# Four 4 KB-row transfers in place of eight 2 KB-row ones at the opening of a two-layer trunk kernel

## The chip, the cores and the metric

The kernel runs on one core of a Trainium2 chip. A core has a matrix engine (TensorE, PE in the profile, with its weight loads as PEld), a vector engine (VectorE, DVE), a scalar engine (ScalarE, ACT), a general engine (GpSimd, POOL), and a sync engine (SyncE, SP) that here only issues transfers. Sixteen DMA engines move data from the chip's main memory (HBM) into the on-chip memory (SBUF). TensorE writes into banks of an accumulator memory (PSUM). Each engine works through its own instruction list in order and waits on semaphores for the others.

The metric is the device time of one execution in microseconds, the median of a few runs.

## The reference

The reference is a trunk of two layers over 256 latent tokens and 256 context tokens of width 1024. Each layer modulates an RMS-normalised stream, projects it, sends it through a convolution branch, an attention branch and gates, and then through a gated MLP. What the change touches is only the very beginning: the first norm, and the first projection that follows it.

```python
def rmsnorm(x, g):
    xf = x.astype(jnp.float32)
    y = xf * lax.rsqrt(jnp.mean(xf * xf, axis=-1, keepdims=True) + EPS)
    return (y * g.astype(jnp.float32)).astype(x.dtype)
...
    s_lat = jax.nn.silu(c)
    s_ctx = jax.nn.silu(c_ctx)
    for l in range(DEPTH):
        mod = (s_lat @ w_ada[l] + b_ada[l])[:, None, :]
        sh1, sc1, g1, sh2, sc2, g2 = jnp.split(mod, 6, axis=-1)
...
        h = modulate(rmsnorm(x, norm1_g[l]), sh1, sc1)
        p = h @ w_in[l]
```

## The kernel before

The stream is kept transposed: eight tiles `x[0]` to `x[7]`, each of 128 channels (partitions) by 512 tokens in float32, the latent tokens (`LAT`) in the first 256 columns and the context tokens (`CTX`) in the last 256. In HBM each tile is a block of 128 rows of 2 KB.

Weights come as units of 128 partitions by 1024 columns in float32 (512 KB, rows of 4 KB). They land in one of four `raw` buffers, ScalarE makes a rounded copy `whi` (L168, L751, L757 and others), VectorE the remainder `wlo` (L169, L754), and every product runs as three matrix products, high by high, high by low and low by high (`mm3`, L187 to L189; for the value projection `v_tile`, L723). For some units the remainder is made by an accumulating transfer that GpSimd issues (L206 to L208).

The opening runs like this:

- SP issues the eight stream tiles (L595), then two units of modulation weights (`wada`, L155), then the first value unit in two halves of 256 KB (`rv`, L747), then the first GLU unit (`rg`, L155), then modulation weights for the next channels.
- The sum of squares over the channels is built pairwise. Even tiles are squared on ScalarE (L606), odd ones on VectorE (L603), which then adds the pair (L604). In the last pair both engines share the odd tile: ScalarE squares its `LAT` half (L598), VectorE its `CTX` half (L599), and VectorE adds each half to the even tile's square (L601). TensorE sums each pair over the partitions by products with a column of ones (`sum0`, L590, four products a pair, `CTX` columns first). A product with both operands in plain float32 appears in the trace as two PE instructions.
- Then come the modulation products for the first channels (`ada_half`, L220, two units), ScalarE's copy of them (L239), transposes (L246), the root on VectorE and GpSimd (L366, L368), its transposes (L374), the modulation and gain (L251 to L256), the modulated stream `h` (L388 on VectorE, L389 on ScalarE, L390 on VectorE), and the first value products (L723).
- Filler products `busy(n)` (L137) multiply an identity matrix into a bank that is overwritten later. They keep TensorE at work while it has nothing to do. Eleven stand at the start, two after the first pair's sums, one before the last pair's, two and five further on.

TensorE's order in the opening is fixed by the function `queued`, which makes each piece follow the one before it. Elsewhere the order of each engine's list is set by a scheduler that works from the program's order and its own estimates, so an edit at one place can move a neighbour. Each transfer of SP and ScalarE raises one of eight semaphores in turn (DMAHW0 to DMAHW7 in the lists below), and a transfer is issued only when the last one with the same semaphore has landed. SP issues in order, so what stands behind a waiting transfer waits too.

From k = 1 on, a stage of the opening makes one tile of `h`, its value products and its share of the GLU products, and brings two units of modulation weights for the next tile. The place they land in comes free when TensorE has used the units before. After eight stages the first layer goes on with the query and key units (`T_Q`, `T_K`), whose first loads are issued during the last stages.

Of the kernel before, what the change touches and what calls it, by code (L numbers as in the profile page):

```python
# [8 lines left out]
F32 = mybir.dt.float32  # L9
# [6 lines left out]
P = 128  # L16
D = 1024
KD = D // P
DEPTH = 2
S = 256  # L20
# [24 lines left out]
U_GLU0, U_V, U_IN, U_NA, U_CO, U_WO, U_UP, U_DN = 0, 2, 6, 36, 40, 44, 52, 96  # L45
# [8 lines left out]
def trunk(ctx: ExitStack, tc: tile.TileContext, xt, cvec, crow, wall, wada, params, bias_t, rope_t, out):  # L54
    nc = tc.nc
    pe, act, dve, pool, sp = nc.tensor, nc.scalar, nc.vector, nc.gpsimd, nc.sync
# [3 lines left out]
    xp = ctx.enter_context(tc.tile_pool(name="x", bufs=1))  # L60
    wp = ctx.enter_context(tc.tile_pool(name="w", bufs=1))
    hp = ctx.enter_context(tc.tile_pool(name="h", bufs=1))
    tp = ctx.enter_context(tc.tile_pool(name="tmp", bufs=1))
# [4 lines left out]
    def nm(s):  # L68
        uid[0] += 1
        return f"{s}_{uid[0]}"  # L70
# [6 lines left out]
    def tmp(w=512):  # L77
        return tp.tile([P, w], F32, tag="t", bufs=5, name=nm("t"))
# [56 lines left out]
    def busy(n):  # L135
        for _ in range(n):
            mm = pe.matmul(sl(warm, 0), ident, ident, start=True, stop=True)  # L137
        return mm


    queue = [busy(11)]

    def queued(f, *a):
        with tc.issue_after(queue[-1].ins):
            queue.append(f(*a))
# [171 lines left out]
        dve.scalar_tensor_tensor(a, mod2(l, part, k)[:, :ns], 1.0, g, ALU.add, ALU.mult)  # L317


    x = [xp.tile([P, 2 * S], F32, name=f"x{k}") for k in range(KD)]  # L320

    class SumSq:

# [268 lines left out]

    ada0 = psum("po")
    for k in range(KD):
        sp.dma_start(x[k], xt[k])  # L595
        q = tmp()
        if k == KD - 1:
            act.activation(q[:, LAT], x[k][:, LAT], AF.Square)  # L598
            dve.tensor_tensor(q[:, CTX], x[k][:, CTX], x[k][:, CTX], ALU.mult)  # L599
            for c in (CTX, LAT):  # L600
                dve.tensor_tensor(q[:, c], q[:, c], prev[:, c], ALU.add)  # L601
        elif k % 2:
            dve.tensor_tensor(q, x[k], x[k], ALU.mult)  # L603
            dve.tensor_tensor(q, q, prev, ALU.add)  # L604
        else:
            act.activation(q, x[k], AF.Square)  # L606
        if k % 2:
            if k == KD - 1:
                queued(busy, 1)
            queued(sum0, q, k == 1, k == KD - 1)  # L610
            if k == 1:
                queued(busy, 2)
        prev = q
    for u in range(2):
        queued(ada_half, ada0, u, raw_unit(wada[0, u]))
# [2 lines left out]
    for l in range(DEPTH):  # L618
# [5 lines left out]
        with ExitStack() if last else start as e1a:  # L624
# [75 lines left out]
            with ExitStack() as e1b:  # L700
# [27 lines left out]
                if l == 0:  # L728
# [14 lines left out]
                    rv = wp.tile([P, UW], F32, tag="raw", bufs=4, name=nm("raw"))  # L743
                    wv = [wp.tile([P, UW], F32R, tag=t, bufs=4, name=nm(t)) for t in ("whi", "wlo")]
                    cuts = [slice(i * 512, (i + 1) * 512) for i in range(2)]
                    for c in cuts:
                        sp.dma_start(rv[:, c], wall[l, U_V][:, c])  # L747
                    rg = raw_unit(wall[l, U_GLU0])
                    wg = [wp.tile([P, UW], F32R, tag=t, bufs=4, name=nm(t)) for t in ("whi", "wlo")]
                    with tc.issue_after(lastev[0].ins):  # L750
# [575 lines left out]
```

## Time and profile before

| What | Value |
|---|---|
| median of 3 runs | 1106.7 us (1106.16 to 1108.9) |
| the profiled execution's own time | 1108.29 us |
| its span in the profile | 1106.5 us |
| PE busy | 1094.5 us, 99% of the span |
| first value product starts | 15.76 us |
| stream tiles | 8 transfers of 256 KB, median 4.2 us from issue to landing |
| data moved | 209.26 MB, 189 GB/s in the mean |

All times inside the kernel count from the first instruction. The profiled execution took 1.8 us more than its span, and 1.6 us more than the median of the runs. A busy TensorE is not a TensorE at its peak: where it waits shows in the idle time before a group and in the chain of work that ended last, not in the busy share.

### The profile page before, as it was taken

The numbers are of one execution on the slowest core, as the hardware profiler recorded it, in microseconds if no ns is written. First come the engines' busy times: TensorE is split into PE (matmuls) and PEld (weight loads), VectorE is DVE, ScalarE is ACT, GpSimd is POOL, SyncE is SP. The second block draws the span as 40 slices with busy tenths as digits, with TensorE's granted clock in tenths as the row PEclk, the third lists the DMA queues.
The fourth block names the chain that finished last, engine by engine and source line by source line (L and its number), as shares of the span: only waits on it lengthen the run. The fifth ranks groups of instructions, "written<-read, shape, count | busy, mean of one in ns | idle before, by whom it ended". The sixth has DMA issues, their size and how long they took to land.

```text
span 1106.5 us, 18047 instructions
## 1 busy us (share of the span) xinstructions
PE 1094.5 (99%) x6896; PEld 951.2 (86%) x6896; DVE 896.3 (81%) x1630; ACT 567.9 (51%) x943; POOL 42.9 (4%) x59
## 2 busy tenths in 40 slices
PE   9999999999999999999999999999999999999997
PEld 7787777888889888888888888989889999999997
DVE  5568898989998788888898556789799888988773
ACT  4458767445324544343433223544676667666642
POOL 1011110011000000000000000000000000000000
PEclk9999999999999999999999999999999999999998
DMA  9988673988843445544557656557644484655771
GB/s 364 290 212 224 153 163 106 278 246 221 264 134 115 125 140 173 146 159 153 171 185 225 215 176 191 185 185 210 193 127 142 151 275 151 206 189 176 229 261 57
DMA packets 60230, 209.26 MB, mean 189 GB/s; under 512 B 7280, under 2 KB 7536, under 8 KB 60144
## 3 DMA queue, kind: packets, MB, share of 16 engines
q1 hardware_dynamic: 55104, 190.77, 53.4%
q0 software_dynamic: 4752, 17.30, 8.2%
q8 instruction: 54, 0.88, 0.3%
q14 instruction: 32, 0.26, 0.1%
q10 hardware_dynamic: 288, 0.04, 0.0%
HBM read 187.63 MB, written 1.05 MB: 171 GB/s over the span
## 4 chain that ended last, share of the span: by engine, by line
PE 87%; DVE 4%; ACT 3%; DMA 3%; SPq 1%; issue 1%; DVEq 0%; ACTq 0%
PE main L187 25%; PE main L189 25%; PE main L188 25%; PE main L723 4%; DMA raw<-in_wall 2%; SPq L715 1%; PE sc L187 1%; PE sc L188 1%; PE sc L189 1%; DVE wlo L169 1%; PE po L220 1%; PE po L563 1%; ACT whi L168 1%; DVE cb L659 1%; PE sc L480 1%
## 5 line engine op out<-in xcount | busy, mean ns | idle before, releaser
L187 PE MATMUL main<-h,whi 128*128 128x256 f32 (+1 forms) x1328 | 447.3, 337 | 0.0
L189 PE MATMUL main<-h,wlo 128*128 128x256 f32 (+1 forms) x1328 | 443.5, 335 | 1.2 <-DVE wlo L169 1.1
L188 PE MATMUL main<-h,whi 128*128 128x256 f32 (+1 forms) x1328 | 442.5, 334 | 0.1
L168 ACT CAST whi<-raw 128x1024 fp32r<-128x1024 f32 (+1 forms) x211 | 217.7, 1036 | 243.2 <-DMA raw<-in_wall 120.3
L169 DVE TENSOR_TENSOR wlo<-raw,whi 128x1024 fp32r<-128x1024 f32 (+1 forms) x211 | 253.1, 1207 | 90.8 <-ACT whi L168 87.7
L187 PEld LDWEIGHTS main<-h,whi 128*128 128x128 f32 x1328 | 249.5, 188 | 30.4 <-issue 2.2
L189 PEld LDWEIGHTS main<-h,wlo 128*128 128x128 f32 x1328 | 249.4, 188 | 30.2 <-DVE wlo L169 2.0
L188 PEld LDWEIGHTS main<-h,whi 128*128 128x128 f32 x1328 | 249.8, 188 | 28.5 <-DVE h L390 0.5
L659 DVE SCALAR_TENSOR_TENSOR cb<-u,par,cb 128x512 f32<-128x512 f32 (+1 forms) x240 | 144.2, 618 | 2.8
L187 PE MATMUL main<-fh,whi 128*128 128x256 f32 (+1 forms) x386 | 123.0, 319 | 0.0
L188 PE MATMUL main<-fl,whi 128*128 128x256 f32 (+1 forms) x386 | 122.9, 318 | 0.0
L189 PE MATMUL main<-fh,wlo 128*128 128x256 f32 (+1 forms) x386 | 122.9, 318 | 0.0
L293 DVE CUSTOM_DVE_ANT_0 t<-raw,sb,par 128x1024 bf16<-128x1024 f32 x72 | 91.5, 1279 | 0.3 <-ACT sb L273 0.3
L188 PEld LDWEIGHTS main<-fl,whi 128*128 128x128 f32 x386 | 72.7, 188 | 5.6
L189 PEld LDWEIGHTS main<-fh,wlo 128*128 128x128 f32 x386 | 72.7, 188 | 5.6
L187 PEld LDWEIGHTS main<-fh,whi 128*128 128x128 f32 x386 | 72.7, 188 | 5.5
L1053 ACT ACTIVATE t<-main,par 128x512 f32<-128x512 f32 (+1 forms) x82 | 50.8, 669 | 37.6 <-PE main L189 37.6
L293 DVE CUSTOM_DVE_ANT_0 t<-own,sb,par 128x1024 bf16<-128x1024 f32 x48 | 60.4, 1280 | 1.7 <-DMA own<-in_wada 1.7
L206 ACT CAST whi<-raw 128x1024 fp32r<-128x1024 f32 x33 | 34.6, 1050 | 49.8 <-PE main L188 42.3
L1054 DVE SCALAR_TENSOR_TENSOR t<-main,par,t 128x510 f32<-128x510 f32 (+1 forms) x82 | 47.6, 616 | 9.4 <-ACT t L1053 9.1
L1057 DVE SCALAR_TENSOR_TENSOR t<-main,par,t 128x510 f32<-128x510 f32 (+1 forms) x82 | 46.7, 611 | 0.0
L389 ACT ACTIVATE h<-t,mod 128x256 fp32r<-128x256 f32 x56 | 25.1, 501 | 34.8 <-DVE t L388 34.7
(215 smaller groups left out, 1262.9 us busy)
## 6 DMA issues: line engine op xcount, KB each, us to landing
raw<-in_wall SPq DMA_DIRECT2D x239, 512.0 KB, 4.3
raw<-in_wada SPq DMA_DIRECT2D x64, 512.0 KB, 4.5
wlo<-raw POOLq DMA_DIRECT2D x33, 512.0 KB, 5.2
own<-in_wada SPq DMA_DIRECT2D x24, 512.0 KB, 5.6
bias<-in_bias_t SPq DMA_DIRECT2D x8, 520.0 KB, 5.3
row<-in_wada SPq DMA_DIRECT2D x8, 512.0 KB, 4.8
sb<-in_crow SPq DMA_DIRECT2D x5, 512.0 KB, 5.0
x<-in_xt SPq DMA_DIRECT2D x8, 256.0 KB, 4.2
```

What stands on the lines that cost most here:

```text
L168: act.copy(hi[:, c], r[:, c])
L169: dve.tensor_tensor(lo[:, c], r[:, c], hi[:, c].bitcast(F32), ALU.subtract)
L187: pe.matmul(ps, w[0], xh, start=start, stop=False)
L188: pe.matmul(ps, w[0], xl, start=False, stop=False)
L189: pe.matmul(ps, w[1], xh, start=False, stop=stop)
L206: act.copy(hi, r)
L293: dve.tensor_tensor_reduce(tmp().bitcast(BF16), r, v, 1.0, pr(l, BADA + n, 1), ALU.mult, ALU.add, mods[l][:, n, s : s + 1])
L659: dve.scalar_tensor_tensor(cb[j], src, w, cb[j], ALU.mult, ALU.add)
L723: mm = pe.matmul(pv[t], h1[n == 1][k][:, c], w[n == 2][:, b], start=k + n == 0, stop=k == KD - 1 and n == 2)
L1053: act.activation(c, pv_, AF.Identity, bias=pr(l, FDB + t, 1), scale=w[1])
L1054: dve.scalar_tensor_tensor(c[:, :, 1:], pv_[:, :, : S - 1], w[0], c[:, :, 1:], ALU.mult, ALU.add)
L1057: dve.scalar_tensor_tensor(c[:, :, : S - 1], pv_[:, :, 1:], w[2], c[:, :, : S - 1], ALU.mult, ALU.add)
```

## The change

The stream arrives as four tiles of two channel blocks each, with rows of 4 KB; the host lays the input out to match, and `x[k]` becomes a view of half a tile. The first value unit comes in one transfer of 512 KB. The first burst of fillers shrinks from eleven to eight, the one after the first pair's sums from two to one, and the one before the last pair's sums goes. The square of tile 6 goes to a buffer of its own (`ss`) in place of one of the five rotating ones.

```diff
-    queue = [busy(11)]
+    queue = [busy(8)]
...
-    x = [xp.tile([P, 2 * S], F32, name=f"x{k}") for k in range(KD)]
+    x2 = [xp.tile([P, 2, 2 * S], F32, name=f"x{k}") for k in range(KD // 2)]
+    x = [t[:, i] for t in x2 for i in range(2)]
...
     for k in range(KD):
-        sp.dma_start(x[k], xt[k])
-        q = tmp()
+        if k % 2 == 0:
+            sp.dma_start(x2[k // 2].rearrange("p i t -> p (i t)"), xt[k // 2])
+        q = tp.tile([P, 512], F32, tag="ss", name=nm("ss")) if k == KD - 2 else tmp()
...
         if k % 2:
-            if k == KD - 1:
-                queued(busy, 1)
             queued(sum0, q, k == 1, k == KD - 1)
             if k == 1:
-                queued(busy, 2)
+                queued(busy, 1)
...
-                    for c in cuts:
-                        sp.dma_start(rv[:, c], wall[l, U_V][:, c])
+                    sp.dma_start(rv, wall[l, U_V])
...
-        "xt": np.ascontiguousarray(xs.T.reshape(KD, P, 2 * S)),
+        "xt": np.ascontiguousarray(xs.T.reshape(KD // 2, 2, P, 2 * S).transpose(0, 2, 1, 3)).reshape(KD // 2, P, 4 * S),
```

On SP, the list from the last stream tiles to the first GLU unit, with the semaphores waited for. `raw_169` and `raw_175` (now `raw_156` and `raw_162`) are the first modulation units, `raw_234` (now `raw_221`) is the value unit, `raw_239` (now `raw_225`) the GLU unit. Before:

```order
L595 DMA x_115<-in_xt 128x512
L595 DMA x_116<-in_xt 128x512 [waits DMAHW0_49]
L595 DMA x_117<-in_xt 128x512 [waits DMAHW1_49]
L155 DMA raw_169<-in_wada 128x1024 [waits DMAHW2_49]
L155 DMA raw_175<-in_wada 128x1024 [waits DMAHW3_49]
L747 DMA raw_234<-in_wall 128x512 [waits DMAHW4_49]
L747 DMA raw_234<-in_wall 128x512 [waits DMAHW5_49]
L155 DMA raw_239<-in_wall 128x1024 [waits DMAHW6_49]
```

And now:

```order
L597 DMA x_107<-in_xt 128x1024
L597 DMA x_108<-in_xt 128x1024
L597 DMA x_109<-in_xt 128x1024
L597 DMA x_110<-in_xt 128x1024
L155 DMA raw_156<-in_wada 128x1024
L155 DMA raw_162<-in_wada 128x1024
L746 DMA raw_221<-in_wall 128x1024 [waits DMAHW0_49]
L155 DMA raw_225<-in_wall 128x1024 [waits DMAHW1_49]
```

No stream tile waits for an earlier transfer any more; the first that does is the value unit, for the first of ScalarE's two small loads (`cv`).

On TensorE, the same stretch from the first pair's sums to the last pair's. Before:

```order
L590 MATMUL pt_118<-one,t_124 128x128 x3
L137 MATMUL sc_96<-ident 128x128 x2
L590 MATMUL pt_118<-one,t_137 128x128 [waits DVE_49]
L590 MATMUL pt_118<-one,t_137 128x128 x3
L590 MATMUL pt_118<-one,t_148 128x128 [waits DVE_49]
L590 MATMUL pt_118<-one,t_148 128x128 x3
L137 MATMUL sc_96<-ident 128x128
L590 MATMUL pt_118<-one,t_159 128x128 [waits DVE_49]
L590 MATMUL pt_118<-one,t_159 128x128 x3
```

And now:

```order
L591 MATMUL pt_111<-one,t_116 128x128 x3
L137 MATMUL sc_96<-ident 128x128
L591 MATMUL pt_111<-one,t_127 128x128 [waits DVE_49]
L591 MATMUL pt_111<-one,t_127 128x128 x3
L591 MATMUL pt_111<-one,t_137 128x128 [waits DVE_49]
L591 MATMUL pt_111<-one,t_137 128x128 x3
L591 MATMUL pt_111<-one,t_147 128x128 [waits DVE_49]
L591 MATMUL pt_111<-one,t_147 128x128
L591 MATMUL pt_111<-one,t_147 128x128 [waits DVE_49]
L591 MATMUL pt_111<-one,t_147 128x128
```

Beside the fillers that are gone, the last pair's four products now wait in two steps, for the `CTX` half's sum and then for the `LAT` half's, where one wait stood ahead of all four.

Later in the opening the scheduler places some loads and ScalarE instructions otherwise. On ScalarE, in the stage that makes `h[6]` (`h_187`, now `h_174`); `whi_689` and `whi_738` (now `whi_675` and `whi_724`) are the first query and key units, `t_606` (now `t_592`) is the copy of the modulation products for the last channels. Before:

```order
L206 CAST whi_689<-raw_687 128x1024 [waits DMAHW4_49]
L207 ACTIVATE wlo_690<-whi_689 128x1024 [waits Activation_49]
L206 CAST whi_738<-raw_736 128x1024 [waits DMAHW0_49,PE_49]
L389 ACTIVATE h_187<-t_586,mod_108 128x256 [waits DVE_49] x2
L207 ACTIVATE wlo_739<-whi_738 128x1024 [waits PE_49,Activation_49]
L239 COPY t_606<-po_593 128x256 [waits PE_49]
```

And now:

```order
L206 CAST whi_675<-raw_673 128x1024 [waits DMAHW1_49]
L207 ACTIVATE wlo_676<-whi_675 128x1024 [waits Activation_49]
L390 ACTIVATE h_174<-t_572,mod_105 128x256 [waits DVE_49] x2
L206 CAST whi_724<-raw_722 128x1024 [waits DMAHW3_49,PE_49]
L239 COPY t_592<-po_579 128x256 [waits PE_49]
L207 ACTIVATE wlo_725<-whi_724 128x1024 [waits Activation_49]
```

The second cast moved from ahead of `h` to behind it, and the copy now stands ahead of `wlo_725`. On SP, three loads stand further back than before: the second half of the value unit for k = 4 and 5 (behind four modulation loads), the depthwise parameters `par` (behind the next two), and the first query unit (behind the last two).

## The prediction

> **What bounds the kernel now.** I read the page first, then the chain of waits of the opening, then the transfers there. The page says that TensorE is the bound almost everywhere:
>
> ```profile
> PE 1094.5 (99%) x6896; PEld 951.2 (86%) x6896; DVE 896.3 (81%) x1630; ACT 567.9 (51%) x943; POOL 42.9 (4%) x59
> PE 87%; DVE 4%; ACT 3%; DMA 3%; SPq 1%; issue 1%; DVEq 0%; ACTq 0%
> ```
>
> PE is busy 99% of the span and carries 87% of the chain that ended last. So what the opening gains or loses moves everything behind it by the same amount, as long as nothing later waits for something that did not move along. The exception to PE's lead is the opening itself (start, duration, what):
>
> ```profile
> 0.74 3.07 DMA cv<-in_cvec
> ...
> 4.20 5.42 DMA x<-in_xt
> ...
> 10.15 0.77 DVE t L601 x2
> ...
> 10.97 1.16 PE pt L590 x8
> 12.13 1.00 PE po L220 x16
> ...
> 15.20 0.52 ACT h L389
> 15.76 2.09 PE main L723 x8
> ```
>
> The path to the first value product at 15.76 is the stream's last transfer, landing at 4.20 + 5.42 = 9.62, then squares and adds, the sums, the modulation products, `h`. The chain's first piece is the load `cv`: the seventh stream tile could only be issued once it had landed at 3.81.
>
> What the transfers moved from 4 to 8 us, when it was all stream, and from 13 to 17 us, when it was all rows of 4 KB; and in between, from 11 to 12 us, when most packets were the value unit's 2 KB rows:
>
> ```profile
> DMA packets 739, 1.32 MB, mean 331 GB/s; under 512 B 96, under 2 KB 96, under 8 KB 739
> DMA packets 460, 1.68 MB, mean 420 GB/s; under 512 B 50, under 2 KB 50, under 8 KB 460
> DMA packets 198, 0.39 MB, mean 393 GB/s; under 512 B 22, under 2 KB 22, under 8 KB 198
> ```
>
> The stream came at 331 GB/s, the weights behind it at 420. But the third row warns: 2 KB rows can run at 393, so row length alone explains about 7% of a gap of 27%; the rest is the stream's own, whether it is the late issue of its last two tiles or something that stays.
>
> **The stream.** The second tile, which completes the first pair, was issued at 1.18 and landed 3.2 later, at 4.38:
>
> ```profile
> 1.18 0.42 SPq L595 DMA_DIRECT2D x<-in_xt  x1
> x<-in_xt SPq DMA_DIRECT2D x1, 256.0 KB, 3.2
> 5.15 0.43 SPq L155 DMA_DIRECT2D raw<-in_wada  x1
> raw<-in_wada SPq DMA_DIRECT2D x1, 512.0 KB, 7.0
> ```
>
> I let the first new transfer land there too. Three more of 524,288 bytes follow. At 420 GB/s they take 1.25 us each, and the last lands at 8.1; at the stream's own 331 GB/s they take 1.58, and it lands at 9.1. I take 8.6, the middle, because one known cause of the slow rate goes (no tile waits for `cv`) and the rows get longer, but neither is shown to be all of it. So the last landing comes 1.0 earlier, with bounds of 0.5 and 1.5.
>
> [...]
>
> **Behind the last landing.** The last two tiles now land together, so ScalarE squares tile 6 after the landing, where before it had done so ahead of it (the first row is the first pair's add, needed further down):
>
> ```profile
> 5.45 0.69 DVE L604 TENSOR_TENSOR t<-t,t 128x512 f32<-128x512 f32 x1
> 9.06 0.63 ACT L606 ACTIVATE t<-x 128x512 f32<-128x512 f32 x1 [1.50 <-DVE t L604]
> 9.71 0.42 ACT L598 ACTIVATE t<-x 128x256 f32<-128x256 f32 x1
> 10.15 0.76 DVE L601 TENSOR_TENSOR t<-t,t 128x256 f32<-128x256 f32 x2
> 13.51 0.62 ACT L751 CAST whi<-raw 128x512 fp32r<-128x512 f32 x1
> ```
>
> Before, from landing to the end of the last add: 10.15 + 0.76 - 9.62 = 1.29. Now: 0.09 to start (as 9.62 to 9.71), 0.65 for tile 6's square (9.06 to 9.71), 0.42 for the half square of tile 7, some 0.06 of handing over, and the last add's 0.38: 1.60. That costs 0.31. The sums give more back. Before, all eight product passes stood behind the last add, 10.97 to 12.13 in the chain, 1.16. Now the `CTX` half's four can run before it and only the `LAT` half's four are left, half of that, 0.58. Gain 0.58. Net 0.27.
>
> So the sums end 1.0 + 0.27 earlier, 1.25 in round numbers, at 10.9. Three things must keep up. The second modulation unit landed at 5.15 + 7.0 = 12.15; two units behind the stream's last it now lands at 8.6 + 2.5 = 11.1, and its half of the products would start at 10.9 + 0.5 = 11.4: just in time, and if the rate is lower, both move together. The value unit as one transfer lands one unit later, at 12.35. ScalarE's cast of its first half started at 13.51, which would be 12.26 now, so it starts 0.1 late; it takes 0.62, and ScalarE's next work is `h`, at 15.20 - 1.25 = 13.95. Hidden by a microsecond; without that cover it would cost its lateness.
>
> **The fillers.** The profile's rows of PE:
>
> ```profile
> 1.84 5.06 PE L137 MATMUL sc<-ident 128*128 128x128 f32 x22 [1.84 <-POOL ident masks.py:199]
> 6.70 1.44 PE L590 MATMUL pt<-one,t 128*128 128x128 f32 x8
> 7.98 0.61 PE L137 MATMUL sc<-ident 128*128 128x128 f32 x4
> 8.42 1.95 PE L590 MATMUL pt<-one,t 128*128 128x128 f32 x16
> 10.21 0.39 PE L137 MATMUL sc<-ident 128*128 128x128 f32 x2
> 10.97 1.16 PE L590 MATMUL pt<-one,t 128*128 128x128 f32 x8 [0.37 <-DVE t L601]
> ```
>
> The same kind of pass takes (6.70 - 1.84) / 22 = 0.22 us at first and (10.21 - 8.42) / 16 = 0.11 later; the change comes inside the row at 6.70, about 7.5. TensorE starts at half rate and reaches full rate after some 5.7 us without a pause. Six passes less in the first burst are 1.3 us less, the two other cuts two passes each. None was on the path: PE still idled 0.37 before the last pair's sums. What they leave is a hole. Eight fillers end near 5.5, and the first pair's add ends at 5.45 + 0.69 = 6.14, as before, since the pair lands at the same time. So PE pauses some 0.6 us in a stretch that had no pause. I cost this at nothing: 0.6 in 5.7 is a small share, and the pause of 0.37 before 10.97 did not bring the half rate back. What it costs if this is wrong is the second rival.
>
> **The moved loads.** These lie behind the opening's first stages:
>
> ```profile
> 18.48 3.86 SPq L155 DMA_DIRECT2D raw<-in_wada  x4
> 27.23 0.80 SPq L155 DMA_DIRECT2D raw<-in_wada  x2
> par<-in_params SPq DMA_DIRECT2D x1, 352.0 KB, 7.6
> 33.59 0.62 ACT L168 CAST whi<-raw 128x512 fp32r<-128x512 f32 x1
> 50.65 0.35 ACT L239 COPY t<-po 128x256 f32<-128x256 f32 x1
> 52.82 0.38 PE L246 MATMUL pt<-ident,t 128*128 128x128 f32 x2
> 61.73 0.55 DVE L657 TENSOR_SCALAR cb<-u,par 128x512 f32<-128x512 f32 x1
> ```
>
> The half value unit goes behind the four loads that end at 22.34. With the slowest landing here, 7.6, it is there by 30.4, and its cast ran at 33.59. `par` goes behind the pair at 27.23, so it lands by 36; the first convolution tap that reads it ran at 61.73. The query unit goes behind the last pair. That one touches ScalarE's copy at 50.65, which now stands behind the second cast; its reader on PE ran at 52.82, so a unit later by one transfer, 1.25, is still covered by 1.8. I take zero for all, up to 0.5 us of loss for the last.
>
> **Sum.** The profiled execution took 1108.29, span 1106.5 and 1.8 around it. Less 1.25 that is 1107.0. That execution lay 1.6 above the median of 1106.7, so against the median I predict 1105.5. A difference of 0.3%, 3.3 us here, is about what a measurement of this kernel can tell from no change, so the forecast is within it.
>
> **Rivals.**
> - *The stream comes no faster.* For it: 331 against 393 GB/s at the same row length, which the change may leave as it is. Then the last landing is at 9.1 to 9.6, and the gain 0.7 to 0.2: 1106.2. Chance 0.17.
> - *The pause keeps TensorE at half rate.* For it: an unbroken run of 5.7 us came before the change of rate. Then every pass costs 0.22: the first pair's eight run 6.2 to 7.9, the one filler left to 8.3, the next pairs' to 10.0 and 11.7, the last's to 13.4, where before they were done at 12.13. If the rate rises midway, the sums end some 0.3 late, near 1107.0; if not before the modulation products (1.0) are through at double length, 2.3 late, 1109.0. Against it: the 0.37 pause. Chance 0.22; I put it at 1107.4. [...]
> - *Half rate into the value products: slower.* If it also holds over the transposes and fillers (two fillers and six transposes, ten passes, 1.1) and the first eight value products (2.09 in their row, so about another 1.7), the sum is 2.3 + 1.1 + 1.7 = 5.1 late, 1111.8. It decides once the half rate lasts past about 16 us. Against it: by then PE has had 9 us of nearly unbroken work. Chance 0.05.
> - *More than the opening gains: faster by over 0.3%.* The waits of PE in the whole span, beyond opening and end:
>
> ```profile
> PE main L189 <- DVE wlo L169: 1.1, 2, 0.6
> PE sc L480 <- ACT pT L552: 0.5, 1, 0.5
> ```
>
> Were both, 1.6, and as much again in smaller ones to vanish with the shift, the time is 1106.7 - 1.25 - 3.2 = 1102.3; from 2.1 on it is over 0.3%. Nothing in the change reaches them directly. Chance 0.08.
>
> **How the numbers follow.** The forecast has 0.48. Its own range is 1105.0 to 1106.0 by the stream's bounds. The first two rivals fill 1106 to 1108 and are within 0.3% too, but for the far end of the second, to which I give 0.02. So: faster 0.08, same 0.48 + 0.17 + 0.20 = 0.85, slower 0.05 + 0.02 = 0.07. The range 1104.2 to 1108.4 leaves out the ends beyond 0.3% and little more; the runs before alone spread over 2.7.
>
> **What would show it.** Right: the last stream transfer lands near 8.6, the last adds end 1.6 behind it, only four sum passes stand behind them, the sums end near 10.9, the first value product starts near 14.5, and pass lengths still halve before 8 us. Wrong: passes of 0.22 us beyond 9 us (the half rate), a last landing past 9.1 (the stream), or a wait of ScalarE's second query cast past 50.4 that reaches PE. What I do not see is a new wait in the attention of the first layer, where the order of transfers could fall out differently.

## The result, and the profile after

The changed kernel is slower: 1108.94 us in the median (22 runs) against 1107.16 us for the kernel before (22 runs beside it), a ratio of 1.0016 with a 95% interval of 1.0009 to 1.0022, or 1.8 us. That is less than the 0.3% taken as the bound of what can be told, but with this many runs it is told from no change, and it lies above the predicted 1104.2 to 1108.4. The profiled execution took 1109.78 us, its span 1108.0. The forecast had gone by the kernel before's median of 1106.7 from three runs; the 22 runs put it at 1107.16.

The page of after, PE's row of busy time and the chain's shares by engine:

```profile
PE 1094.2 (99%) x6886; PEld 951.1 (86%) x6886; DVE 896.1 (81%) x1630; ACT 568.0 (51%) x943; POOL 43.1 (4%) x59
PE 90%; DVE 4%; ACT 3%; DMA 2%; issue 1%; DVEq 0%; ACTq 0%; SPq 0%
```

TensorE does the same work in the same time. The difference is in the opening. The chain that ended last, of after (start, duration, what):

```profile
0.74 0.41 ACTq L117
1.18 5.03 DMA par<-in_params
6.39 0.61 DVE t L605
7.10 0.70 DVE t L606
7.85 1.16 PE pt L591 x8
9.01 0.26 PE sc L137 x2
9.27 4.45 PE pt L591 x24
13.72 1.00 PE po L220 x16
...
17.30 2.11 PE main L723 x8
```

The stream is no longer in the chain. The first value product starts at 17.30 in place of 15.76, 1.54 later, and the profiled times differ by 1.49. What leads the chain now is `par`, 28 KB of parameters that ScalarE issues at 1.18. The issues of the first two microseconds, before and then after (the last two numbers are KB and us from issue to landing; with several transfers, the median):

```profile
x<-in_xt SPq DMA_DIRECT2D x3, 256.0 KB, 3.2
par<-in_params ACTq DMA_DIRECT2D x1, 28.0 KB, 3.4
cv<-in_cvec ACTq DMA_DIRECT2D x1, 8.0 KB, 3.1
```

```profile
x<-in_xt SPq DMA_DIRECT2D x3, 512.0 KB, 4.8
par<-in_params ACTq DMA_DIRECT2D x1, 28.0 KB, 5.0
cv<-in_cvec ACTq DMA_DIRECT2D x1, 8.0 KB, 4.1
```

Two loads that the change does not touch take 1.0 and 1.7 us longer; `par` lands at 6.21 in place of 4.55. Their packets and the stream's from 2 to 4 us, before and then after (packets, MB, share of the engines; q1 is SP's queue, q10 ScalarE's):

```profile
q1 hardware_dynamic: 310, 0.58, 84.0%
q10 hardware_dynamic: 274, 0.03, 11.0%
```

```profile
q1 hardware_dynamic: 145, 0.55, 75.4%
q10 hardware_dynamic: 119, 0.01, 3.9%
```

The stream moves nearly as many bytes in these two microseconds as before, in half as many packets, and the small loads get through less than half of theirs. Before and after, the two queues moved packets in similar numbers (310 and 274, then 145 and 119). On the stream's queue that is 0.58 MB / 310 = 1.9 KB a packet before and 0.55 MB / 145 = 3.8 KB after, about a row each time. How the engines divide themselves between the two queues no run shows.

VectorE waits for `par`. Its rows of before, and then of after (start, duration, engine, line, operation, names, and in brackets the idle time ahead and what ended it):

```profile
4.57 0.16 DVE L250 SCALAR_TENSOR_TENSOR wb<-par 128x1 f32<-128x1 f32 x1 [3.57 <-DMA par<-in_params]
4.65 0.69 DVE L603 TENSOR_TENSOR t<-x 128x512 f32<-128x512 f32 x1
```

```profile
6.23 0.16 DVE L250 SCALAR_TENSOR_TENSOR wb<-par 128x1 f32<-128x1 f32 x1 [5.22 <-DMA par<-in_params]
6.31 0.69 DVE L605 TENSOR_TENSOR t<-x 128x512 f32<-128x512 f32 x1
...
9.90 0.69 DVE L606 TENSOR_TENSOR t<-t,t 128x512 f32<-128x512 f32 x1
10.51 0.42 DVE L601 TENSOR_TENSOR t<-x 128x256 f32<-128x256 f32 x1
11.03 0.76 DVE L603 TENSOR_TENSOR t<-t,ss 128x256 f32<-128x256 f32 x2
```

In both kernels an instruction of one column, L250 (the gain's constant part, needed ten microseconds later), stands ahead of VectorE's first square. Before it cost little, because `par` landed at 4.55, only 0.2 behind the first pair, and VectorE later waited for the last tile anyway. Now VectorE starts at 6.31 though the first pair has been there since 4.65, and from there it works without a gap: 1.40 us a pair, then the halves, until 11.79. The last tile has been there since 8.54.

TensorE waits in turn. Its rows of after:

```profile
1.84 3.78 PE L137 MATMUL sc<-ident 128*128 128x128 f32 x16 [1.84 <-POOL ident masks.py:199]
7.85 1.16 PE L591 MATMUL pt<-one,t 128*128 128x128 f32 x8 [2.22 <-DVE t L606]
8.85 0.43 PE L137 MATMUL sc<-ident 128*128 128x128 f32 x2
9.25 4.47 PE L591 MATMUL pt<-one,t 128*128 128x128 f32 x24
13.65 1.07 PE L220 MATMUL po<-raw,sil 128*32 128x256 f32 x16
```

The pause is 2.22 us, and the 24 sum passes take 4.47, some 0.19 each, where they had taken 0.11 to 0.12. The granted clock shows why. It reads 1.00 at the very start too, where passes take 0.21, so the first rise has to be read from the passes; a later fall does show in it. Stretches of after (from:to, length, busy time and count of PE, PEld, DVE, ACT, POOL, then the granted clock, DMA share, GB/s), and one of before for the second:

```profile
5.64:9.05 3.41, 1.20 (x10) 1.19 (x10) 2.61 (x5) 1.75 (x4) 0.00 (x0) 1.00 1.03 423
9.06:12.47 3.41, 3.41 (x17) 3.23 (x16) 2.52 (x6) 0.56 (x2) 0.00 (x0) 0.50 1.03 423
12.60:16.00 3.40, 3.40 (x38) 2.66 (x37) 0.44 (x3) 0.89 (x2) 1.03 (x1) 1.00 1.02 417
```

```profile
9.10:12.40 3.30, 2.93 (x30) 2.53 (x32) 1.35 (x4) 1.01 (x2) 0.00 (x0) 1.00 1.03 408
```

TensorE reached full rate at 5.64 (where the trace's clock record starts; passes took 0.21 up to 5.20 and 0.11 from 8.06), was busy for 1.20 of the next 3.41 us, and lost the rate for the 3.41 us after that, in which the sums of the second and third pair fell, 16 of the 24 passes. The last pair's eight ran at full rate again. The last sums ended 0.7 us later behind the last add than before (13.65 - 11.79 against 12.06 - 10.92).

Behind the opening little changes: the same products, matched in order between the two traces, start 1.55 us later at 14 us, 1.73 at 102 us, 1.58 at 886 us and 1.14 at TensorE's last product; the spans differ by 1.5.

### The profile page after: what moved, and what is told of

Same layout as the page of the kernel before. It is cut to its first block, busy times and chain, and to the rows that moved or that the text cites. A ratio compares the mean times of both kernels' runs of the same rounds, so it can differ in the third digit from the quotient of the medians.

```text
span 1108.0 us, 18021 instructions
## 1 busy us (share of the span) xinstructions
PE 1094.2 (99%) x6886; PEld 951.1 (86%) x6886; DVE 896.1 (81%) x1630; ACT 568.0 (51%) x943; POOL 43.1 (4%) x59
## 3 DMA queue, kind: packets, MB, share of 16 engines
q0 software_dynamic: 4752, 17.30, 8.1%
HBM read 187.63 MB, written 1.05 MB: 170 GB/s over the span
## 4 chain that ended last, share of the span: by engine, by line
PE 90%; DVE 4%; ACT 3%; DMA 2%; issue 1%; DVEq 0%; ACTq 0%; SPq 0%
PE main L187 26%; PE main L189 26%; PE main L188 26%; PE main L723 4%; DMA raw<-in_wall 2%; PE sc L187 1%; PE sc L189 1%; PE sc L188 1%; PE po L220 1%; PE po L564 1%; ACT whi L168 1%; DVE wlo L169 1%; DVE cb L659 1%; PE sc L481 1%; PE pt L591 1%
```

## The experiments

All kernels were compared with the kernel before on the same chip. Its median there was 1106.80 to 1107.53, so a row is judged by its ratio, which differs from the quotient of the two medians by up to 0.0005. "Value" is the start of the first value product in the profiled execution, "adds" the end of VectorE's last add, "last x" the landing of the last stream tile; all in us.

| Kernel | median | ratio to before [95%] | par | last x | adds | value |
|---|---|---|---|---|---|---|
| before | 1107.16 | 1 | 4.55 | 9.62 | 10.92 | 15.76 |
| after | 1108.94 | 1.0016 [1.0009, 1.0022] | 6.21 | 8.54 | 11.79 | 17.30 |
| r1_before_again | 1107.22 | 1.0002 [0.9993, 1.0011] | 4.40 | 9.19 | 10.48 | 15.33 |
| r3_after_again | 1109.06 | 1.0020 [1.0011, 1.0029] | 5.97 | 8.28 | 11.56 | 16.89 |
| e1_old_fillers | 1108.06 | 1.0008 [0.9999, 1.0017] | 6.03 | 8.37 | 11.62 | 16.33 |
| e5_long_fillers | 1108.20 | 1.0016 [1.0007, 1.0025] | 5.73 | 8.18 | 11.31 | 15.80 |
| e2_small_late | 1106.56 | 0.9998 [0.9989, 1.0007] | 5.93 | 8.23 | 9.88 | 14.37 |
| e2_small_late_again | 1105.94 | 0.9992 [0.9983, 1.0000] | 6.14 | 8.46 | 10.15 | 14.64 |
| e10_only_l250_late | 1107.34 | 1.0001 [0.9992, 1.0009] | 5.95 | 8.28 | 10.16 | 14.65 |
| e3_small_late_old_fillers | 1106.98 | 0.9999 [0.9990, 1.0008] | 6.17 | 8.50 | 10.16 | 15.09 |
| e4_before_few_fillers | 1107.19 | 1.0004 [0.9995, 1.0012] | 4.45 | 8.85 | 10.14 | 14.98 |
| e6_value_unit_only | 1106.38 | 0.9994 [0.9985, 1.0003] | 4.52 | 9.37 | 10.66 | 15.50 |
| e7_small_first_on_sp | 1107.75 | 1.0008 [1.0000, 1.0017] | 3.87 | 9.46 | 10.95 | 16.26 |
| e8_four_of_2kb | 1108.22 | 1.0009 [1.0000, 1.0018] | 5.27 | 9.03 | 10.86 | 15.35 |
| v1_last_pair_split | 1107.77 | 1.0006 [0.9997, 1.0015] | 5.95 | 8.47 | 9.77 | 15.84 |
| e9_before_late_par | 1107.95 | 1.0011 [1.0003, 1.0020] | 4.55 | 9.06 | 10.35 | 15.48 |
| e12_control_read_only | 1108.00 | 1.0014 [1.0005, 1.0023] | 4.55 | 9.23 | 10.80 | 15.74 |
| e11_before_par_behind_silu | 1111.13 | 1.0037 [1.0023, 1.0050] | 7.24 | 9.14 | 12.56 | 19.13 |

### Repeats: how far one trace goes

> The kernel before once more, to see how typical its first profile was (that execution took 1108.29 us, 1.1 to 1.5 above the median of its runs, and its stream tiles landed last at 9.62 with gaps of 1.15 and 1.43 us between some of them, 0.64 between others). If the slow stream was a draw: the last tile lands near 8.8 to 8.9, as in the kernel before with few fillers, and the first value product starts near 15.0. If it is typical: 9.6 and 15.8. The ratio must come out at 1.000 within its interval.

> A third look at the kernel before, for the same question: last stream tile at 8.8 to 8.9 if the first profile was a slow draw, at 9.6 if it was typical.

> The changed kernel once more, beside the others on one chip: 1.5 to 1.9 us above the kernel before. The clock theory expects passes of 0.21 us somewhere between 8 and 13 us in this trace too, either because the full rate is lost again, as in the first profile, or because it comes late; the first adds on VectorE end near 7.7 as before. Small loads alone: full rate throughout and still the same time.

The third look at before (1107.14) had its last tile at 8.96, its adds' end at 10.52, its value product at 15.36. So the profiled execution that the prediction was built on was a late draw: 9.62 against 9.19 and 8.96. TensorE's full rate came late in it too: passes went from 0.21 to 0.11 near 7.5, against 5.6 and 5.1 in the two others (their 22 filler passes took 4.47 and 4.28, not 5.06). The repeat of before lay 0.4 above the median beside it (1106.82), which shows how far two medians of one kernel differ. The changed kernel repeats with its loss (2.2, above the 1.5 to 1.9 expected), its pause (2.26) and its half rate.

### The readers of the small loads moved back

The theory: VectorE's wait for `par` delays the whole opening, and the pause that follows costs TensorE its clock. `e2_small_late` keeps the change whole and puts ScalarE's reader of `cv` and VectorE's reader of `par` (L250) behind the squares (`lastsq` is ScalarE's half square of tile 7, `lastadd` VectorE's last add).

```diff
-    act.activation(sil[:, : 2 * KD], cv.rearrange("p k s -> p (k s)"), AF.Silu)
...
+    with tc.issue_after(lastsq.ins):
+        act.activation(sil[:, : 2 * KD], cv.rearrange("p k s -> p (k s)"), AF.Silu)
...
-            dve.scalar_tensor_tensor(first, pr(0, BADA + KD, 1), 1.0, g, ALU.add, ALU.mult)
+            with tc.issue_after(lastadd.ins):
+                dve.scalar_tensor_tensor(first, pr(0, BADA + KD, 1), 1.0, g, ALU.add, ALU.mult)
```

> The changed kernel with its few fillers; the two instructions that read the small loads (the first gain's half on VectorE, the activation of the condition on ScalarE) moved behind the squares, so that nothing in the stream's squares waits for a small load. Small loads: the first adds end near 6.4, the last near 10.2, the sums near 10.8, the first value product near 14.5, time 1.2 us below the kernel before. Clock: a pause of about 0.8 us (5.6 to 6.4) stays. If any pause ahead of the first sums costs the full rate, the sums end at 12 or later and the time is 0 to 1.5 us above the kernel before; if only a long one does, the result is that of the small loads.

> The changed kernel with both readers of the small loads behind the squares, a second time, on another chip, to see whether the 1.0 us by which its first value product started earlier than in the kernel before (14.37 against 15.33 to 15.76) reaches the time. If the opening passes through: value product at 14.2 to 14.6 again and 1105.8 to 1106.5, 0.5 to 1.2 us below the kernel before. If it is given back later: 1106.6 to 1107.2.

VectorE and TensorE in the second of the two runs:

```profile
4.66 0.69 DVE L605 TENSOR_TENSOR t<-x 128x512 f32<-128x512 f32 x1 [3.65 <-DMA x<-in_xt]
...
9.39 0.76 DVE L603 TENSOR_TENSOR t<-t,ss 128x256 f32<-128x256 f32 x2
10.07 0.15 DVE L250 SCALAR_TENSOR_TENSOR wb<-par 128x1 f32<-128x1 f32 x1
```

```profile
6.21 1.16 PE L591 MATMUL pt<-one,t 128*128 128x128 f32 x8 [0.58 <-DVE t L606]
...
9.00 2.05 PE L591 MATMUL pt<-one,t 128*128 128x128 f32 x16 [0.24 <-DVE t L606]
10.99 1.07 PE L219 MATMUL po<-raw,sil 128*32 128x256 f32 x16
```

`par` is as late as in the changed kernel (6.14 against 6.21) and the stream as early (8.46 against 8.54), but VectorE starts with the first pair, the pause is 0.58, the granted clock stays at 1.00 (5.70 to 12.40), and the value product comes 2.66 us earlier. The loss is gone: the intervals of both runs lie wholly below after's. The two traces share so much that they divide the 2.66: the adds end 1.64 earlier, and the sums end 1.02 sooner behind them (0.84 against 1.86). Against before the gain isn't settled: the value product is some 0.7 to 1.0 earlier than in the repeat of before, the medians 0.2 and 1.1 lower, and both intervals reach 1.

One run moved L250 alone (the same edit without the `sil` lines):

> The changed kernel with VectorE's reader of par alone moved behind the squares; ScalarE's reader of cv stays ahead of its squares, few fillers. cv lands with the first tile (4.6 against 4.4), so if par alone holds the opening this does as well as moving both: adds end at 9.9 to 10.3, first value product 14.4 to 14.9, time 1106.2 to 1107.0. If cv's reader on ScalarE counts as well, the adds end at 10.5 or later and the time is 1107.2 or more.

```profile
4.44 0.69 DVE L606 TENSOR_TENSOR t<-x 128x512 f32<-128x512 f32 x1 [3.43 <-DMA x<-in_xt]
5.48 0.69 DVE L607 TENSOR_TENSOR t<-t,t 128x512 f32<-128x512 f32 x1 [0.35 <-ACT t L609]
```

Its opening is as good as the second `e2` trace's (adds 10.16, value 14.65). VectorE's first add waits 0.35 for ScalarE, which waits for `cv`; that is all `cv` costs here. The median, 1107.34, is 0.3 above what I expected of that and would by itself have spoken for `cv`; the interval does not separate it from before, and it ends at 1.0009, where after's begins and below the repeat's (from 1.0011).

### The fillers

`e1` gives the changed kernel its old fillers back, `e5` makes only the first burst long, `e3` joins old fillers to `e2`, `e4` gives the few fillers to the kernel before.

```diff
-    queue = [busy(8)]
+    queue = [busy(19)]   # e5; e1 and e3: busy(11) and the two later bursts as before
```

> The changed kernel with the old fillers (eleven, two, one); the transfers stay changed. Two theories for the 1.8 us that the change lost. Clock: PE's pause of 2.2 us ahead of the first sums put TensorE back to half rate from 9.1 to 12.5; with the fillers the pause shrinks to under 1 us, the full rate holds, the sums end near 12.4 as VectorE's late adds (11.8) allow, the first value product starts near 16.1, and the time is 0.3 us above the kernel before. Small loads: VectorE starts late (6.3) because the small parameter load lands late, and that is all; the fillers change nothing, the first value product stays near 17.3, and the time stays 1.6 to 1.8 us above the kernel before.

> The changed kernel with nineteen fillers in the first burst in place of eight, so that PE works until the late first adds at 7.7 whichever rate it has; the rest of the fillers stay few. Clock: the full rate comes once and stays, the sums end near 12.4, the time is that of the old fillers or up to 0.5 us less: 0.3 to 1.2 above the kernel before. If the full rate comes late the fillers themselves end near 10 and the sums behind them are late by up to 1 us. Small loads alone: no change against the changed kernel, 1.8 above.

> Both at once: the changed transfers, the readers of the small loads behind the squares, and the old fillers. Either theory: PE has no pause, VectorE starts at 4.7, the last adds end near 10.2, the first value product starts near 14.5, and the time is 1.0 to 1.4 us below the kernel before, if what the opening gains goes through to the end.

> The kernel before with the changed kernel's few fillers and nothing else. The pause ahead of the first sums is then about 0.5 us (5.6 to 6.2), since the small loads land early. Clock, if any pause counts: half rate in part of the runs, time 0.3 to 1.5 us above the kernel before, with a wider spread. Clock, if only a pause of some 2 us counts, and small loads: the same time as the kernel before, within 0.2 us.

TensorE in `e5`, ahead of and in its sums:

```profile
1.84 6.16 PE L137 MATMUL sc<-ident 128*128 128x128 f32 x38 [1.84 <-POOL ident masks.py:199]
7.84 1.06 PE L591 MATMUL pt<-one,t 128*128 128x128 f32 x8
...
12.15 1.07 PE L220 MATMUL po<-raw,sil 128*32 128x256 f32 x16
```

With the pause filled, the rate stays full (granted clock 1.00 from 5.70 to 12.40) and the sums end 0.84 behind the last add, as in `e2`, while VectorE is still held (5.73) and its adds still end late (11.31). So half rate and hold are two costs in the traces. The fillers of before shorten the pause to 1.54 in `e1` and keep the rate too (1.00 from 5.18 to 12.00), and the value product starts at 16.33. In the times the share of the half rate is not shown: `e1` (1.0008) lies about halfway, but its interval overlaps both before's level and after's, and `e5` (1.0016) gained nothing. Few fillers alone, in the kernel before, where VectorE is not held, cost nothing that can be told (`e4`, 0.4 above before's median, the interval across 1); the pause there is 0.47.

`e3` missed its forecast of 14.5 and of a time 1.0 to 1.4 below before: the value product started at 15.09, the time was level (1106.98 against 1106.80). Its adds ended at 10.16, as in `e2`, but its full rate came late, near 7.5, its first fillers ran into the first sums (5.06 for 22 passes), and TensorE then worked without a pause until the sums ended at 11.43, 0.44 later than in `e2`. With VectorE free, the old fillers can hold the opening up.

`e5`'s median stayed at 1108.2 although its value product is as early as in the profiled run of before; this stays open (below).

### The other parts

`e6` makes the first value unit's single transfer (in place of two) alone in the kernel before. `e7` issues `cv` and `par` on SP ahead of the stream. `e8` keeps the four transfers and gives them rows of 2 KB. `v1` adds to `e3` two transfers for the last pair, and TensorE sums two squares one by one, so that VectorE need not add them. They were meant to be the last pair's, but `KD - 3` is the third pair; the last pair's adds stayed on VectorE behind the last landing.

```diff
-    act.dma_start(cv, cvec)
+    sp.dma_start(cv, cvec)                       # e7, and the same for par
...
-            sp.dma_start(x2[k // 2].rearrange("p i t -> p (i t)"), xt[k // 2])
+            sp.dma_start(x2[k // 2], xt[k : k + 2].rearrange("i p t -> p i t"))   # e8
...
+            if k == KD - 3:                      # v1
+                queued(sum0, prev, False, False)
+            else:
+                dve.tensor_tensor(q, q, prev, ALU.add)
```

> The kernel before with one part of the change, the first value unit in one transfer in place of four. Every theory that puts the loss into the small loads and the fillers expects no change: last tile at 8.85 to 9.6, first value product 14.9 to 15.8, time within 0.2 us of the kernel before (1106.9 to 1107.3). If the single transfer costs the value products a later start, they begin up to 1 us after the sums' line L220 ends as against before, and the time is 0.3 to 1 us above.

> The changed kernel with cv and par issued on SP ahead of the stream; everything else as changed, the few fillers too. Theory of the late small load: par lands by about 3.0 to 3.5 us in place of 5.0 to 6.2, VectorE's L250 no longer waits, and VectorE adds a pair as soon as it is there; the two issues ahead push the stream back by 0.5 to 1.2 us, so its last tile lands at 9.1 to 9.7 and the adds end at 10.2 to 10.8 (changed kernel: 11.3 to 11.8). First value product at 14.6 to 15.6, time 1106.5 to 1107.5: clearly below the changed kernel's 1109. Rival, the loss lies with the fillers alone and par's landing costs nothing: the value product stays near 16.9 to 17.3 and the time at 1108.5 to 1109.5.

> The changed kernel with its four transfers, issued as quickly, few fillers, but their rows 2 KB long as before. It tells apart why par lands late. Theory A, the length of the rows in front of par's small packets: par lands at 4.4 to 4.8 as in the kernel before, VectorE starts with the first landing, the last tile lands at 8.6 to 9.4, the adds end at 10.0 to 10.6, first value product 14.8 to 15.6, time 1106.5 to 1107.4, clearly below the changed kernel. Theory B, the quicker issue (all four transfers and the next weights are queued by 3.7 us, where eight took until 4.6): par lands at 5.2 to 6.2 with rows of 2 KB too, the adds end at 11.0 to 11.8, value product 16.2 to 17.3, time 1108 to 1109.2.

> The changed kernel with the readers of cv and par behind the squares and the old number of fillers, and besides the last two tiles as two transfers of 256 KB, whose squares TensorE sums one by one, so that VectorE adds nothing after the last landing. If VectorE's own chain (three pairs at 1.40 us, then the halves) is what ends the opening once the stream is quick: the adds end at 9.6 to 9.9 in place of 10.16, the first value product at 14.5 to 14.8, time 1106.2 to 1106.8, 0.3 to 0.7 us below the kernel before. If the stream still sets the end: nothing gained, 1106.8 to 1107.4.

`e6` came 0.5 below the time I expected, with an interval that reaches 1 and a value product as in before: no change that can be told. In `e7` `par` lands at 3.87 and VectorE starts with the first pair, but that pair comes 0.8 later (5.44); the time is between before and after, 0.25 above the range I gave, and the value product (16.26) is 0.7 later than the latest I expected. Its TensorE rows show one cost I had not counted:

```profile
7.01 2.08 PE L591 MATMUL pt<-one,t 128*128 128x128 f32 x8 [1.38 <-DVE t L606]
```

Passes of 0.26 in the mean: the full rate came only at 10.39 here. It had not yet come when the pause began.

`e8` does not decide cleanly. `par` lands at 5.27, at the early end of theory B's forecast, 4.1 us after its issue against 3.4 before and 5.0 after (4.40 to 4.55 in the seven traces with before's transfers and an issue of `par` by 1.24, 5.73 to 6.21 in the eight with the changed ones); the value product, at 15.35, is where theory A had it, and the median again B's. So, by this one trace, the length of the rows is one part of `par`'s delay, and the quicker issue of larger transfers another. And the stream itself: its tiles of 512 KB land every 1.32 us with rows of 2 KB ((9.03 - 5.07) / 3) and every 1.30 with rows of 4 KB ((8.54 - 4.65) / 3). That is 397 and 404 GB/s. Between landings, then, the rows made no difference. But the first tile of `e8` landed at 5.07 and not at 4.65 (SP's queue moved 0.38 MB from 2 to 4 us, in after 0.55), and its last at 9.03, within the 8.85 to 9.62 of before's eight transfers. So this trace doesn't show the earlier last landing without the long rows, and nothing here separates the missing waits from the size of the transfers.

`v1` missed: the adds end at 9.77, in the range forecast though the third pair's add and not the last pair's was left out, but TensorE has eight passes more, works through its sums without a gap until 12.2, and becomes the bound.

### The late load alone, in the kernel before

`e9` was to issue `par` later in the kernel before, and to read it ahead of VectorE's first square. It issued no later (at 1.24 against 1.18, during the table load of 1.28 us ahead of ScalarE's Silu), so it tells nothing of a late `par` and serves as a control; `e12` is the same kernel again. `e11` makes the transfer wait for a write of ScalarE behind its Silu:

```diff
+    held = dve.tensor_scalar(small([P, 1], "held", 1), par[:, :1], 1.0, None, ALU.mult)   # e9, e11, e12
...
     act.activation(small([P, 1], "wb", 4), one, AF.Silu)
+    act.activation(par[:, :1], one, AF.Silu)     # e11 alone
+    act.dma_start(par[:, :DW], params[:, :DW])
...
+            with tc.issue_after(held.ins):
+                dve.tensor_tensor(q, x[k], x[k], ALU.mult)
```

> The kernel before (eight transfers, old fillers) with the suspected cause alone put in: ACT issues par behind its first Silu, some 2 us later, and one small read of par stands ahead of VectorE's first square. Theory of the held VectorE: par lands at 5.8 to 6.8 in place of 4.5, VectorE starts there and needs its 5.4 us, so the adds end at 11.4 to 12.2 (before: 10.5 to 10.9), the first value product starts at 16.2 to 17.2 (before: 15.3 to 15.8), and the time is 0.8 to 1.8 us above the kernel before. Rival, the loss of the change lies in the long rows or the fillers themselves: the time stays within 0.4 us of the kernel before.

> The control: the kernel before with the small read of par ahead of VectorE's first square and par's transfer on time, a second time. Expected: par at 4.4 to 4.7, adds end at 10.2 to 10.7, value product 15.2 to 15.6, time within 0.4 us of the kernel before; if its first median, 0.9 us above, was no draw, again 0.6 to 1.2 above.

> The run before with this aim issued par no later (its transfer started beside the Silu and landed at 4.55), so it said nothing of a late par. Here ScalarE first writes one column of par after its first Silu and the transfer has to wait for that. Everything else as in the control beside it, which is the kernel before with one small read of par ahead of VectorE's first square. Theory of the held VectorE: par lands at 5.8 to 6.6, VectorE starts there, the adds end at 11.3 to 12.1 (control: 10.3 to 10.6), the value product starts at 16.1 to 17.0 (control 15.3 to 15.6), the time is 0.7 to 1.6 us above the control. Rival, VectorE's hold is caught up by the opening's other work: value product and time within 0.3 us of the control.

VectorE, TensorE and two stretches in `e11`, with eight transfers of 2 KB rows and the old fillers:

```profile
7.35 0.15 DVE L595 TENSOR_SCALAR held<-par 128x1 f32<-128x1 f32 x1 [6.35 <-DMA par<-in_params]
...
11.79 0.76 DVE L603 TENSOR_TENSOR t<-t,t 128x256 f32<-128x256 f32 x2
```

```profile
1.84 5.06 PE L138 MATMUL sc<-ident 128*128 128x128 f32 x22 [1.84 <-POOL ident masks.py:199]
9.37 1.16 PE L591 MATMUL pt<-one,t 128*128 128x128 f32 x8 [2.46 <-DVE t L607]
```

```profile
7.01:10.42 3.41, 1.05 (x9) 1.06 (x10) 3.07 (x6) 1.10 (x2) 0.00 (x0) 1.00 1.02 395
10.43:13.84 3.41, 3.41 (x18) 3.41 (x18) 2.03 (x6) 0.56 (x2) 0.00 (x0) 0.50 1.03 411
```

`par` landed later than I meant, at 7.24, and the whole picture of the changed kernel comes back larger: VectorE held, a pause of 2.46, the full rate lost for 3.41 us. The value product is 3.4 later than in the control (19.13 against 15.74), the median (of 5 runs) 3.1 higher. No long rows, no smaller bursts of fillers are needed: a late `par` ahead of VectorE's squares is enough. One thing else differs from before in all three kernels: VectorE squares the second pair's odd tile before it makes the first add, so the first sums start later. In `e12`, whose fillers are through at 6.05, this makes a pause of 1.55, and TensorE keeps its rate (mean granted clock 0.998, against 0.995 in `e11`); the comparison of `e11` with the control is free of it, but not all of the 2.46 comes from `par`.

### What stays open

The control's median is 0.9 to 1.0 above before in both runs, and `e5`, `e8` and `v1` lie 0.7 to 1.4 above it, though the value product starts at before's 15.3 to 15.8 in their traces. The rest of the profiled executions, from that product on, takes 1090.9 to 1092.8 us, a spread as large as the loss. The granted clock of the other executions says a little more. It is 0.996 or less in 14 of the 33 executions of the changed kernel and in none of the 143 of before that ended within 1109 us; 3.41 us at half rate, as in the trace of after, are 0.0015 of the span, so by this estimate these 14 lost the rate. But in `e5`, `v1` and `e9` no execution is below 0.997, so what lifts their medians is not a rate lost after its rise. And in the 22 runs of after, those at 0.997 or more took as long as the others (1108.9 and 1109.0 in the mean). A rate that comes late would not show there: `e7`'s profiled execution, with its rise at 10.39, reads 0.997. Whether it came late in them no trace shows. So medians of these kernels are read only against differences larger than about 1 us, and the landings, holds and pauses from the traces.

## Why the prediction was wrong

- *What bounds the kernel.* Right: the opening's loss of 1.54 reached the end of the profiled execution (spans 1.5 apart).
- *The stream.* Right in what it did: the last transfer landed at 8.54, forecast 8.6. Wrong in the base: the 9.62 it was compared with was a late draw, the latest of eight traces with those transfers. Their mean is 9.18, that of eight traces with the changed kernel's transfers 8.36, so the gain was 0.8 rather than 1.0, within the bounds. The doubt I had drawn from the row with 393 GB/s was right in part: between landings the rows made no difference in `e8`, 397 GB/s for 2 KB against 404 for 4 KB; for the whole stream `e8` leaves it open, since its last tile came at 9.03.
- *"The first pair's add ends at 5.45 + 0.69 = 6.14, as before, since the pair lands at the same time."* This is the step that failed. The pair landed at 4.65, a little late, but the add ended at 7.79, because L250 stood ahead of the square and waited for `par` until 6.21. I followed only transfers that the diff names. The row of before was there to be read: VectorE's first row had waited for `par`, not for the stream, and started 0.08 ahead of the first square. What stood at no slack at all had to be priced when the packets ahead of it doubled in size (1.9 to 3.8 KB).
- *Behind the last landing.* ScalarE's squares went as worked out (8.57 and 9.23 to 9.65), and the last sums waited in two steps. But even unheld, VectorE needs 5.5 us from the first pair to the last add (4.66 to 10.15 in `e2`), so the adds end near 10.15 whenever the last tile lands before some 8.8. That floor I did not see; with it the forecast of 10.2 for the adds holds in `e2` by accident (in after they ended at 11.79), and a still earlier stream gains nothing. The 0.58 for the sums was too much: in `e2` they ended 0.84 behind the last add, before 1.14, a gain of 0.30, because the third pair's passes, begun at 9.00, were only just through when the last pair's could start.
- *The fillers, "I cost this at nothing".* Wrong as an outcome, by the step above: the pause was 2.22 and not 0.6. With 0.58 (`e2`) the forecast of nothing is right, and the few fillers alone cost nothing that can be told in `e4`. The unbroken run of 5.7 us that I measured the pause against was a draw of that one execution, 3.7 and 3.3 in the two others. The second rival had a part of the mechanism, half rate in the sums, and 1107.0 to 1109.0; in the traces this cost 1.02 of the 2.66, and it came with a pause nearly four times as long as the one I gave it (2.22 against 0.6). That its far end, 1109.0, is the measured time is luck: it has no held VectorE in it.
- *The moved loads.* Right: nothing. The shift between the traces is the same at 14 and at 886 us but for 0.2.

Put together from the traces, against the repeat of `e2`: a hold of 1.64 and a half rate of 1.02 turn a kernel that is level with before, or up to 1 us better, into one that is 1.8 slower. That the hold starts the loss is shown by moving its reader away (`e10`, `e2`) and by putting a late `par` into the kernel before (`e11`); how the loss divides is shown for single executions only.

## What to carry to other kernels

When transfers at the opening get larger, look for the small loads on other queues that run beside them (here `par`, 5.0 us from issue to landing in place of 3.4), and for who reads those loads: a reader of one column ahead of a busy engine's first work makes its load the start of the whole path. In the profile of before such a load shows as the last releaser of an engine's first row, with next to no slack to the next one (0.08 us here). Move the reader back to where its result is needed before making the stream faster, and then count the working time of the engine behind the stream, which may end last anyway.

## What the runs showed of the hardware that was not expected

TensorE's full rate, once reached, was lost again in three traces. In after the granted clock reads 1.00 from 5.64, 0.50 from 9.06 and 1.00 again from 12.47; in its repeat 1.00 from 4.95 to 8.36 and 0.50 from there to 11.77; in `e11` 1.00 from 7.01 to 10.42 and 0.50 from 10.43 to 13.84. In the 3.41 us ahead of the fall PE was busy for 1.20, 1.15 and 1.05, with a pause of 2.22, 2.26 and 2.46. In `e1` and `e8`, with pauses of 1.54 and 1.29, PE was busy for 1.87 and 2.54 of 3.41 us, and the clock stayed at 1.00. The rows of `e1` and of `e8`:

```profile
5.18:8.59 3.41, 1.87 (x17) 1.68 (x16) 2.32 (x5) 1.76 (x4) 0.00 (x0) 1.00 1.01 414
```

```profile
6.08:9.49 3.41, 2.54 (x18) 2.16 (x18) 3.11 (x5) 1.70 (x3) 0.00 (x0) 1.00 1.06 418
```

Whether the pause or the busy share decides, or something else, these runs do not show: both differ between the two groups. Nor do they show what sets the moment of the first rise: it came at 5.64 in after, near 7.5 in before, near 5.6 and 5.1 in before's two repeats, and only at 10.39 in `e7` (16 passes from 6.98 to 10.39, then 37 from 10.50 to 13.80), though TensorE's work began at 1.84 in after, in before and in `e7` alike.

A load of 28 KB on ScalarE's queue took 3.2 to 3.4 us beside rows of 2 KB issued on SP's in eight pieces (4.5 in `e11`, where it was issued at 2.79 and not by 1.24), 4.1 beside the same rows in four (one trace), and 4.5 to 5.0 beside rows of 4 KB in four.
